# Attention units of 64 queries of two heads with 192 keys, in place of 128 queries of one head with 256

## The chip, the core and the metric

The kernel runs on one core of a Trainium2 chip. The core has five engines that run beside each other, each with its own queue: TensorE (PE, with its weight loads PEld), VectorE (DVE), ScalarE (ACT), GpSimd (POOL) and SyncE (SP), which issues the DMAs. The metric is the device time of one execution in microseconds (us); lower is better.

## The reference

A model of four layers over 1040 tokens (16 meta tokens and 1024 others) with 1024 features: sliding-window attention, mLSTM, HGRN2, and sliding-window attention again. Each layer adds its branch to the residual stream. The attention branch, which the change concerns, is, with 16 query heads, 4 key heads, head size 64, blocks of 128 queries and a window of 128 keys:

```python
s = jnp.einsum('bnqhgd,bnkhd->bnhgqk', qb, kk) * (A_HD ** -0.5)
dist = (jnp.arange(BLOCK)[:, None] + BLOCK) - jnp.arange(2 * BLOCK)[None, :]
band = (dist >= 0) & (dist < A_WIN)
s = jnp.where(mask[None, :, None, None], s, -jnp.inf)
m = jnp.maximum(s.max(axis=-1), sink)
e = jnp.exp(s - m[..., None])
p = e / (e.sum(axis=-1) + jnp.exp(sink - m))[..., None]
o = jnp.einsum('bnhgqk,bnkhd->bnqhgd', p, vv)
```

Here `kk` holds the 256 keys of a block and of the block ahead of it. Of these a query sees its own position and the 127 ahead of it; 64 neighbouring queries together see 191.

## The kernel before, in words

All layers hold the activations transposed: features on the partitions, tokens along the free dimension, in chunks of 400, 384 and 256 tokens (first chunk with the 16 meta tokens). Values are fp32; the large products are made of three `float32r` matmuls over a high and a low part (`split`, L193; `proj`, L211; `proj_out`, L293). Nine blocks cut the tokens: block 0 is the 16 meta tokens, blocks 1 to 8 have 128 tokens each.

*The order.* TensorE's order is written out by hand: every layer makes a list of steps (cost, function, early work), and `weave` (L56) lays two lists into each other by their costs, so that attention steps stand between projection matmuls. The costs are numbers in the code. The other engines' order is decided by a scheduler when the program is built; steps under `hi` (L286) have priority there.

*The attention layer* (`layer_a`, L416, for the first and the last layer). Queries of two heads come out of a projection in one tile t (64 features of each head on 128 partitions). `qk_proj` (L486) takes them through a scale, squares, a rotation by DMA and the rope; `stat_q` (L506) sums the squares of each query with one matmul per block (L516: 128 query columns as the stationary operand, 2 columns of ones moving), and ScalarE turns the sums into `rq` (L518, L519). `q_split` (L453) writes for each head a tile `qs` with the high part on one half of the partitions and the low part on the other (L463, L464).

`mixers` (L595) makes units out of (pair of tiles, block, head half hh). A unit holds two heads, u = 0 and 1, one from each tile of the pair, and has three steps, which run two units apart (`T_LAG`, `V_LAG`: T two and V four units behind S):

- `S_step` (L598): for each head two matmuls (keys' high and low part, L621 and L622) give scores of 128 queries by 256 keys, [128, 2, 256] in one PSUM bank. VectorE adds the mask, multiplies, and takes the minimum (L629), ScalarE takes the exponential and its sum (L632), VectorE the reciprocal (L634), GpSimd multiplies (L635). GpSimd also puts the sink into column 256 (L626).
- `T_step` (L638): four transposes (L647) turn the probabilities into a PSUM tile `pt` with the keys on the partitions; ScalarE copies the high part `Ph` (L649) and VectorE subtracts the low part `Pl` (L650).
- `V_step` (L652): four matmuls with the values (L666) add up in `po`; after two blocks ScalarE and VectorE put the two halves together (L674, L675).

*PSUM.* There are 8 banks of [128, 512] fp32. All PSUM tiles of all layers come out of `psum` (L145) with one tag and 8 buffers. Tiles named `pt` are those of T_step (L642), of the value tiles of the attention layers (L574), of `gate_turn` in the mLSTM layer, which turns the input and forget gates of a chunk one after the other (L785 to L794), of `s4` there, which turns back each block of a head with two transposes (L937) that VectorE copies out with two copies (L939), of a small turn at L829 and L830, and of the states of the HGRN2 layer (L1211).

Of the kernel before, what the change touches and what calls it, by code (L numbers as in the profile page):

```python
# [9 lines left out]
F32 = mybir.dt.float32  # L10
# [5 lines left out]
P = 128  # L16
# [95 lines left out]
def hybrid_kernel(ctx: ExitStack, tc: tile.TileContext, ins, out, layers=(0, 1, 2, 3)):  # L112
# [32 lines left out]
    def psum(tag, bufs):  # L145
        return ps.tile([P, 512], F32, tag="p", name=nm(tag), bufs=8)
# [269 lines left out]
    def layer_a(i, j, first, last, fin):  # L416
# [4 lines left out]
        def enter():  # L421
            R["mix"] = mix = new_mix()
            R["masks"] = masks = mix.tile([P, 384], F32, name=nm("masks"))
            sp.dma_start(masks, ins["a_masks"])
            R["cons"] = cons = mix.tile([P, 18], F32, name=nm("cons"))
            sp.dma_start(cons, ins["a_cols"][j])
            v.tensor_scalar(cons[:, 0:1], cons[:, 0:1], -0.125, None, op0=ALU.mult)
            v.tensor_scalar(cons[:, 2:18], cons[:, 2:18], -1.0, None, op0=ALU.mult)

        order = {}  # L430

# [21 lines left out]
        def q_split(t):  # L453


            def step(qf, n, c0, cn):
                def fn():
                    q = qf()
                    R["q", t, n] = []
                    for hh in range(2):  # L460
                        st = R["mix"].tile([P, CHUNKS[n][1]], F32R, tag=f"qs{n}", name=nm("qs"), bufs=4)
                        hs, os = slice(64 * hh, 64 * hh + 64), slice(64 - 64 * hh, 128 - 64 * hh)
                        s.copy(st[hs, :cn], q[hs])  # L463
                        v.tensor_tensor(st[os, :cn], q[hs], st[hs, :cn].bitcast(F32), op=ALU.subtract)  # L464
                        R["q", t, n].append(st)
# [20 lines left out]
        def qk_proj(src, gcol, work, fsplit, ch, t=None):  # L486
# [11 lines left out]
            def finish(n, c0, cn):  # L498
# [7 lines left out]
                def stat_q():  # L506

                    sq = late[n][1]
                    nb = len(CHUNK_BLOCKS[n])
                    R["rq", t, n] = rq = R["mix"].tile([P, 2 * nb], F32, tag=f"rq{n}", name=nm("rq"), bufs=4)  # L510
                    st = psa()
                    for k, b in enumerate(CHUNK_BLOCKS[n]):
                        if last and b == 0:
                            continue
                        q0 = blk(b)[0] - c0
                        pe.matmul(st[:, 2 * k : 2 * k + 2], sq[:, q0 : q0 + P], R["masks"][:, 0:P:64], start=True, stop=True)  # L516
                    z = slice(2 if last and n == 0 else 0, 2 * nb)
                    s.activation(rq[:, z], st[:, z], AF.Ln, bias=eps, scale=1.0 / 64)  # L518
                    s.activation(rq[:, z], rq[:, z], AF.Exp, scale=-0.5)  # L519
# [17 lines left out]
                if t is not None:  # L537
                    return [(D_Q[0], [0.0, factors, None]), (D_Q[1], [108 * len(CHUNK_BLOCKS[n]), stat_q, None]),
# [25 lines left out]
        def v_proj(src, jj):  # L564
# [7 lines left out]
            def finish(n, c0, cn):  # L572
                def fn():
                    pt = psum("pt", 1)  # L574
# [20 lines left out]
        def mixers():  # L595


            def S_step(w):  # L598
                mix, cons = R["mix"], R["cons"]
                b, hh, n = w["b"], w["hh"], w["n"]  # L600
                kh, kl = R["k", w["pair"] // 2][hh]
                q0, nq = blk(b)
                qb = slice(q0 - chunks[n][0], q0 - chunks[n][0] + nq)
                kq = CHUNK_BLOCKS[n].index(b)
                if b == 0:
                    k0, kbs = 0, ((0, 0, 16),)
                elif b == 1:
                    k0, kbs = 0, ((0, 0, 16), (1, 16, 128))
                else:
                    k0, kbs = q0 - P, ((b - 1, 0, 128), (b, 128, 128))  # L610
                w["kbs"] = kbs
                nk = sum(z[2] for z in kbs)
                kw, mo = (nk if b == 0 else 256), {0: 128, 1: 112}.get(b, 0)
                kb = slice(k0, k0 + kw)
                S = psum("pm", 2).rearrange("p (u k) -> p u k", u=2)
                w["Sm"] = Sm = mix.tile([P, 2, 257], F32, tag="Sm", name=nm("Sm"), bufs=2)
                st, den = small(2), small(2)
                sinks = []
                for u, t in enumerate(w["ts"]):
                    q = R["q", t, n][hh]  # L620
                    pe.matmul(S[:nq, u, :kw], q[:, qb], kh[:, kb], start=True, stop=False)  # L621
                    pe.matmul(S[:nq, u, :kw], q[:, qb], kl[:, kb], start=False, stop=True)  # L622
                    head = (2 * (t // 4) + hh) * 4 + t % 4
                    sinks.append(cons[:nq, 2 + head : 3 + head])
                    if u == 0:
                        g.tensor_copy(Sm[:nq, :, nk : nk + 1], cons[:nq, 2 + head : 4 + head].rearrange("p (u c) -> p u c", c=1))  # L626
                for u in range(2):
                    rq = R["rq", w["ts"][u], n][:nq, 2 * kq + hh : 2 * kq + hh + 1]
                    v.tensor_tensor_reduce(Sm[:nq, u, :nk], S[:nq, u, :nk], R["masks"][:nq, P + mo : P + mo + nk],  # L629
                                           rq, sinks[u], ALU.add, ALU.min, st[:nq, u : u + 1])  # L630
                for u in range(2):
                    s.activation(Sm[:nq, u, : nk + 1], Sm[:nq, u, : nk + 1], AF.Exp, scale=-1.0,  # L632
                                 bias=st[:nq, u : u + 1], accum_out=den[:nq, u : u + 1])
                v.reciprocal(den[:nq], den[:nq])  # L634
# [868 lines left out]
```

## Time and profile before

| | |
|---|---|
| Median of 3 runs | 2619.22 us (2617.09 to 2619.5) |
| The profiled execution | 2615.34 us, span of its instructions 2613.6 us |
| Granted TensorE clock, mean | 0.993 |
| Attention units, first layer and last layer | from 84 to 424 us and from 2213 to 2553 us |
| mLSTM layer alone on TensorE | from 523 to 1560 us |

The span goes from the first instruction's start to the last one's end. Rows of the groups read: line, engine, operation, tile written and tiles read, shapes, count, then busy time in us, mean ns of one, and the engine's idle time ahead of them with what ended it. A form as 128*128 128x256 on TensorE is the stationary operand (rows by columns) and the output. Rows of the timeline begin with the start in us and the duration in us. Rows of the waits read: who waited for whom, us in total, times, longest. A plain fp32 matmul (not `float32r`, not a transpose) leaves two records, an instruction of the others one. Matmuls are pipelined: the next one starts before the record of the one ahead ends, so that start to start is what one costs.

### The profile page before, as it was taken

The page shows a single profiled execution, that of the slowest core. Times are in us where ns is not written, and L with a number is a line of the kernel's source. Part 1 is how long each engine was busy: PE and PEld are TensorE (multiplying, and loading weights), DVE is VectorE, ACT ScalarE, POOL GpSimd, SP SyncE. Part 2 cuts the span into 40 slices and gives each one's busy share as a digit, 9 for nine tenths or more (in the row PEclk, how much of TensorE's full clock was granted, in tenths as well). Part 3 has the DMA queues.
Part 4 walks back from the last instruction along what each step waited for, and adds up shares of the span by engine and source line. Part 5 has one row for each costly group of instructions (what it writes and reads, how often), then busy time and mean ns, then how long its engine had stood idle before and what let it go on. Part 6 is the DMA issues. An engine that isn't in the chain of part 4 may idle for free.

```text
span 2613.6 us, 54261 instructions
## 1 busy us (share of the span) xinstructions
PE 2565.6 (98%) x20422; PEld 2485.5 (95%) x20422; DVE 1952.1 (75%) x5248; ACT 1689.4 (65%) x4422; POOL 249.1 (10%) x502
## 2 busy tenths in 40 slices
PE   7999999999999999999999999999999999999999
PEld 6999999999999999999999999999999999999999
DVE  6797798785647474646465688988888978887996
ACT  6776767576555555554555757878675857767772
POOL 2221221000000000000000000101000000321330
PEclk8999999999999999999999999999999999999999
DMA  4212111021111111111111111111111113112112
GB/s 130 68 51 85 54 44 48 22 66 58 41 58 41 58 41 51 44 53 41 57 41 50 57 32 37 34 34 34 38 38 31 37 51 92 56 47 84 56 40 79
DMA packets 82582, 135.92 MB, mean 52 GB/s; under 512 B 12032, under 2 KB 35712, under 8 KB 82320
## 3 DMA queue, kind: packets, MB, share of 16 engines
q1 hardware_dynamic: 82320, 132.45, 16.3%
q8 instruction: 161, 2.64, 0.4%
q14 instruction: 101, 0.83, 0.1%
HBM read 117.56 MB, written 4.26 MB: 47 GB/s over the span
## 4 chain that ended last, share of the span: by engine, by line
PE 80%; DVE 9%; ACT 6%; DMA 2%; issue 2%; SPq 1%; POOL 0%; DVEq 0%; ACTq 0%; POOLq 0%
PE pj L228 39%; PE pj L322 16%; PE pj L277 10%; PE po L666 2%; PE pt L647 2%; PE po L909 1%; PE pa L923 1%; PE po L911 1%; PE pm L621 1%; ACT Sm L632 1%; PE pm L622 1%; DVE Sm L629 1%; PE pj L273 1%; PE pm L1161 1%; DMA cs<-in_rope 1%
## 5 line engine op out<-in xcount | busy, mean ns | idle before, releaser
L228 PE MATMUL pj<-uh,wh 128*128 128x256 f32 (+2 forms) x2688 | 915.2, 340 | 9.3 <-ACT uh L194 9.2
L228 PE MATMUL pj<-ul,wh 128*128 128x256 f32 (+2 forms) x2688 | 867.7, 323 | 2.1 <-DVE ul L195 1.9
L228 PE MATMUL pj<-uh,wl 128*128 128x256 f32 (+2 forms) x2688 | 864.6, 322 | 0.0
L228 PEld LDWEIGHTS pj<-uh,wh 128*128 128x128 f32 x2688 | 510.0, 190 | 26.0 <-ACT uh L194 12.5
L228 PEld LDWEIGHTS pj<-ul,wh 128*128 128x128 f32 x2688 | 510.1, 190 | 10.5 <-DVE ul L195 5.4
L228 PEld LDWEIGHTS pj<-uh,wl 128*128 128x128 f32 x2688 | 509.7, 190 | 0.0
L195 DVE TENSOR_TENSOR wl<-wr,wh 128x512 fp32r<-128x512 f32 (+1 forms) x338 | 233.6, 701 | 50.1 <-ACT wh L194 47.1
L194 ACT CAST wh<-wr 128x512 fp32r<-128x512 f32 (+1 forms) x338 | 202.9, 613 | 102.1 <-PE pj L322 32.7
L322 PE MATMUL pj<-yh,wh 128*128 128x384 f32 (+2 forms) x768 | 253.2, 330 | 8.2 <-DVE x L325 6.2
L325 DVE TENSOR_TENSOR x<-x,pj 128x384 f32<-128x384 f32 (+2 forms) x480 | 234.6, 507 | 35.0 <-PE pj L322 33.7
L322 PE MATMUL pj<-yh,wl 128*128 128x384 f32 (+2 forms) x768 | 245.5, 320 | 0.0
L322 PE MATMUL pj<-yl,wh 128*128 128x384 f32 (+2 forms) x768 | 245.5, 320 | 0.0
L277 PE MATMUL pj<-wh,uh 128*128 128x256 f32 (+1 forms) x768 | 232.2, 302 | 0.0
L277 PE MATMUL pj<-wl,uh 128*128 128x256 f32 (+1 forms) x768 | 216.5, 282 | 0.0
L277 PE MATMUL pj<-wh,ul 128*128 128x256 f32 (+1 forms) x768 | 216.2, 282 | 0.0
L635 POOL TENSOR_TENSOR Sm<-Sm,s 128x512 f32<-128x512 f32 (+2 forms) x136 | 142.2, 1046 | 450.6 <-DVE s L634 435.8
L632 ACT ACTIVATE Sm<-Sm,s 128x257 f32<-128x257 f32 (+2 forms) x272 | 130.8, 482 | 78.9 <-DVE s L629 74.7
L404 ACT ACTIVATE t<-t 128x384 f32<-128x384 f32 (+2 forms) x240 | 117.9, 491 | 82.9 <-DVE t L403 80.8
L403 DVE SCALAR_TENSOR_TENSOR t<-pj,t 128x384 f32<-128x384 f32 (+2 forms) x192 | 98.7, 514 | 80.1 <-ACT t L402 78.4
L322 PEld LDWEIGHTS pj<-yh,wh 128*128 128x128 f32 x768 | 144.5, 188 | 11.9 <-DVE x L325 7.3
L194 ACT CAST yh<-r 128x384 fp32r<-128x384 f32 (+2 forms) x120 | 57.1, 478 | 152.0 <-PE pj L322 139.9
L277 PEld LDWEIGHTS pj<-wh,uh 128*128 128x128 f32 x768 | 144.6, 188 | 2.2
(255 smaller groups left out, 5434.0 us busy)
## 6 DMA issues: line engine op xcount, KB each, us to landing
wr<-in_b_win SPq DMA_DIRECT2D x124, 256.0 KB, 2.9
wr<-in_a_win SPq DMA_DIRECT2D x80, 256.0 KB, 2.9
wr<-in_c_win SPq DMA_DIRECT2D x64, 256.0 KB, 2.7
wr<-in_a_wout SPq DMA_DIRECT2D x32, 256.0 KB, 2.8
wr<-in_b_wout SPq DMA_DIRECT2D x32, 256.0 KB, 2.8
t<-t SPq DMA_DIRECT2D x104, 48.0 KB, 1.9
cs<-in_rope SPq DMA_DIRECT2D x11, 400.0 KB, 3.4
cs<-in_rope SPq DMA_DIRECT2D x11, 384.0 KB, 3.4
```

Source lines behind the costliest of these rows:

```text
L194: s.copy(h, src)
L195: v.tensor_tensor(l, src, h.bitcast(F32), op=ALU.subtract)
L228: pe.matmul(acc[:, :cn], a[:, k, :], b[:, k, c0 : c0 + cn], start=(k == 0 and i == 0), stop=(k == KT - 1 and i == 2))
L277: pe.matmul(acc[:cn, :nc], a[:, k, c0 : c0 + cn], m[:, kk, :], start=(k == 0 and j == 0), stop=(k == KT - 1 and j == 2))
L322: pe.matmul(acc[:, :cn], a[:, k, mc], b, start=(k == 0 and i == 0), stop=(k == 1 and i == 2))
L325: v.tensor_tensor(x[:, m, c0 : c0 + cn], x[:, m, c0 : c0 + cn], acc[:, :cn], op=ALU.add)
L403: v.scalar_tensor_tensor(a[:, :cn], z, 0.0, a[:, :cn], op0=ALU.min, op1=ALU.subtract)
L404: s.activation(a[:, :cn], a[:, :cn], AF.Exp)
L632: s.activation(Sm[:nq, u, : nk + 1], Sm[:nq, u, : nk + 1], AF.Exp, scale=-1.0, bias=st[:nq, u : u + 1], accum_out=den[:nq, u : u + 1])
L635: g.tensor_tensor(Sm[:nq, :, :nk], Sm[:nq, :, :nk], den[:nq].rearrange("p (u c) -> p u c", c=1).to_broadcast([nq, 2, nk]), op=ALU.mult)
L647: pe.transpose(pt[:kn, ki, u, :nq], Sm[:nq, u, ko : ko + kn], ident[:nq, :nq])
L666: pe.matmul(po[:, :, q0 - g0 : q0 - g0 + nq], V[pair // 2, kb][:kn, P * hh : P * hh + P], w[part][:kn, ki, :, :nq], start=(ki == 0 and par ...
```

## The change

A unit still has two heads, but its rows are now 64 queries of both heads, and its two halves are a = 0 and 1, the first and the last 64 queries of the block. Half a keeps the 192 keys from 128 ahead of its first query on. `q_split` interleaves the two heads by 64 queries in one tile per pair, `stat_q` works by half blocks (64 stationary columns) and writes to partitions 0 to 63 or 64 to 127 by the parity of t, and the sinks and masks are laid out for it. The score matmuls take 256 keys where they exist; the columns that are not used are overwritten or not read. The transposes put the keys of both halves on the partitions of the blocks b - 1 and b; rows that no half sees are zero, from a clearing of `pt` and of two fixed `Sm` tiles at the layer's start. So `pt` in the attention layers is one fixed tile, and `psum` gives the tag `pt` a bank of its own and all others 7. The value tiles' turn uses `psa` instead.

```diff
     def psum(tag, bufs):
-        return ps.tile([P, 512], F32, tag="p", name=nm(tag), bufs=8)
+        if tag == "pt":
+            return ps.tile([P, 512], F32, tag="pt", name=nm(tag), bufs=1)
+        return ps.tile([P, 512], F32, tag="p", name=nm(tag), bufs=7)
...
+            R["pt"] = psum("pt", 1)
+            v.memset(R["pt"], 0.0)
+            R["Sm"] = [mix.tile([P, 2, 257], F32, name=nm("Sm")) for _ in range(2)]
+            for z in R["Sm"]:
+                g.memset(z, 0.0)
...
+                        parts = [(st[:, :ce].rearrange("p (h u q) -> p h u q", u=2, q=64)[:, :, u],
+                                  q[:, meta:].rearrange("p (h q) -> p h q", q=64))]
+                        if meta:
+                            parts.append((st[:, ce + 64 * u : ce + 64 * u + meta], q[:, :meta]))
+                        for z, src in parts:
+                            s.copy(z[hs], src[hs])
+                            v.tensor_tensor(z[os], src[hs], z[hs].bitcast(F32), op=ALU.subtract)
...
-                        pe.matmul(st[:, 2 * k : 2 * k + 2], sq[:, q0 : q0 + P], R["masks"][:, 0:P:64], start=True, stop=True)
...
+                    for k, q0 in enumerate(hv):
+                        pe.matmul(st[us, 2 * k : 2 * k + 2], sq[:, q0 - c0 : q0 - c0 + 64], R["masks"][:, 0:P:64], start=True, stop=True)
...
-                    return [(D_Q[0], [0.0, factors, None]), (D_Q[1], [108 * len(CHUNK_BLOCKS[n]), stat_q, None]),
+                    return [(D_Q[0], [0.0, factors, None]), (D_Q[1], [108 * len(halves(n)), stat_q, None]),
...
-                    pt = psum("pt", 1)
+                    pt = psa()
...
+                for a in range(na):
+                    qa = 2 * (q0 + 64 * a - blk(CHUNK_BLOCKS[n][1 if n == 0 else 0])[0]) if b else 768
+                    qb = slice(qa, qa + nr)
+                    k0, at, kw = q0 + 64 * a - 192, 256 * a, 256
+                    if b < 2:
+                        k0, at, kw = 0, 256 * a + lo[a], 256 - lo[a]
+                    elif k0 < 0:
+                        k0, at = k0 + 64, at + 64
+                    pe.matmul(S[:nr, at : at + kw], q[:, qb], kh[:, k0 : k0 + kw], start=True, stop=False)
+                    pe.matmul(S[:nr, at : at + kw], q[:, qb], kl[:, k0 : k0 + kw], start=False, stop=True)
+                for a in range(na):
+                    c = 2 * hv.index(q0 + 64 * a) + hh
+                    m0 = P + (P if b == 0 else lo[a] - 64)
+                    v.tensor_tensor_reduce(Sm[:nr, a, lo[a] : 256], S[:nr, 256 * a + lo[a] : 256 * a + 256],
+                                           R["masks"][:nr, m0 : m0 + 256 - lo[a]], rq[:nr, c : c + 1],
+                                           sink[:nr], ALU.add, ALU.min, st[:nr, a : a + 1])
...
+                pt = R["pt"].rearrange("p (k a q) -> p k a q", k=2, a=2)
...
+                    parts = [(0, 0, 64, 128), (0, 1, 0, 128)]
+                if b:
+                    parts += [(1, 0, 192, 64), (1, 1, 128, 128)]
+                for ki, a, z, m in parts:
+                    nr = P if b else 64 + NMETA
+                    pe.transpose(pt[:m, ki, a, :nr], Sm[:nr, a, z : z + m], ident[:nr, :nr])
...
+                            pe.matmul(po[:, z0 : z0 + 256], V[pair // 2, kb][:, P * hh : P * hh + P],
+                                      w[part][:, ki], start=(ki == 0 and part == "Ph"), stop=(ki == 1 and part == "Pl"))
```

For blocks 2 to 8 `lo` is (64, 64), so 192 columns of each half are reduced, exponentiated and multiplied; for block 1 it is (176, 112).

More of the change, by code (lines that the diff above doesn't have):

```diff
@@ L611, in S_step @@
[L611 to L616, printed above, removed]
-                st, den = small(2), small(2)
[L618 to L633, printed above, removed]
```

127 lines of the change are left out of this document (70 added, 57 removed).

## The prediction

> **What bounds the kernel now.** I read the page first, then the busy time by stage, then the list of groups with shapes kept apart, then who waited for whom, then the timeline at the places that the diff touches.
>
> ```profile
> span 2613.6 us, 54261 instructions
> ...
> PE 2565.6 (98%) x20422; PEld 2485.5 (95%) x20422; DVE 1952.1 (75%) x5248; ACT 1689.4 (65%) x4422; POOL 249.1 (10%) x502
> ...
> PE 80%; DVE 9%; ACT 6%; DMA 2%; issue 2%; SPq 1%; POOL 0%; DVEq 0%; ACTq 0%; POOLq 0%
> ```
>
> TensorE is busy for 98% and holds 80% of the chain that ended last. So work that is taken from VectorE, ScalarE or GpSimd is worth only what TensorE waits for them, and every wait that TensorE newly gets is paid in full, where it had none. Which of the two holds is read stage by stage (stretch, its length, then PE, PEld, DVE, ACT, POOL busy):
>
> ```profile
> 84.00:490.00 406.00, 399.44 (x2754) 388.21 (x2753) 347.72 (x917) 286.16 (x812) 93.31 (x155) 1.00 0.18 54
> 523.00:1560.00 1037.00, 1036.92 (x6836) 1011.29 (x6835) 644.07 (x1617) 582.98 (x1375) 7.54 (x67) 1.00 0.15 49
> 2213.00:2560.00 347.00, 336.56 (x2343) 330.43 (x2342) 291.25 (x753) 249.07 (x697) 87.26 (x127) 0.99 0.20 60
> ```
>
> The first and the third stretch hold the attention units of the two attention layers: there TensorE idles 6.6 and 10.4 us, 17.0 together, beside a VectorE that is 86% and 84% busy. That is all the room that faster softmax steps have. The middle stretch is the mLSTM layer: TensorE idles 0.08 us in 1037. The diff seems not to touch that layer, but it changes the pool of PSUM banks that it draws from.
>
> **What the change takes away.** A score tile goes from 2x256 to 2x192 keys for VectorE's masked reduction (L629), ScalarE's exponential (L632) and GpSimd's product (L635).
>
> ```profile
> L629 DVE CUSTOM_DVE_ANT_0 Sm<-pm,masks,cons 128x256 f32<-128x256 f32 x224 | 113.7, 539 | 5.0 <-PE pm L622 4.2
> ...
> L629 DVE CUSTOM_DVE_ANT_0 Sm<-pm,masks,cons 128x144 f32<-128x144 f32 x32 | 12.3, 420 | 2.9 <-PE pm L622 2.9
> ```
>
> (mean 539 and 420 ns), and on GpSimd:
>
> ```profile
> L635 POOL TENSOR_TENSOR Sm<-Sm,s 128x512 f32<-128x512 f32 x112 | 126.1, 1126 | 273.7 <-DVE s L634 265.8 <-PE pt L647 5.4 <-PE pm L622 2.2
> ```
>
> 112 columns cost VectorE 539 - 420 = 119 ns, so 64 fewer save 68 ns, times 224 instructions 15 us; ScalarE's exponential loses the same 64 columns; GpSimd's 1126 ns falls by a quarter at most, some 30 us over 112. All three are off the path. Per unit the chain from scores to transposes gets 2x68 + 280 = 0.4 us shorter and a little on ScalarE, against waits of this size:
>
> ```profile
> PE pt L647 <- POOL Sm L635: 2.5, 4, 1.2
> ```
>
> ```profile
> PE po L666 <- DVE v L587: 4.3, 2, 3.6
> ```
>
> The first row (first attention stretch) is the wait that the shorter chain ends; the second (last layer's start) hangs on the value tiles, which no softmax step makes. Bounds: nothing to all 17.0 us. I take 5 us off, because 15 us less in 639 us of VectorE work shortens a queue by 2%, and only the waits on L635 hang on the chain itself.
>
> TensorE itself gets nothing from the 192 keys: the score matmuls are still 4 a unit with 256 keys swept (`kw` is 256), the transposes are still 4, and the product with the values is still 4 times 256 columns. The few matmuls of the meta block and of block 1 differ by under 0.5 us.
>
> **What it adds on TensorE: the query statistic** (`stat_q`, L516). Before, one matmul per block with 128 stationary columns, 136 in all; after, one per half block with 64 columns, 8x17 + 8x16 = 264. An fp32 matmul leaves two records, so 272 records become 528.
>
> ```profile
> L516 PE MATMUL pa<-masks,t 128*128 128x2 f32 x272 | 34.5, 242 | 0.1
> ```
>
> ```profile
> 111.81 0.95 PE L516 MATMUL pa<-masks,t 128*128 128x2 f32 x8
> ```
>
> ```profile
> 84.66 0.17 PE L621 MATMUL pm<-r,qs 128*16 128x16 f32 x1
> ...
> 84.69 0.17 PE L622 MATMUL pm<-r,qs 128*16 128x16 f32 x1
> ```
>
> Eight records with 128 columns take 0.95 us from the first start to the last end, and a short matmul lasts 0.17 (the two rows above): (0.95 - 0.17) / 7 = 112 ns from start to start. With 16 columns it is 84.69 - 84.66 = 30 ns. On the line between them, 64 columns come to 30 + 48/112 x 82 = 65 ns: 528 x 65 = 34.3 us against 272 x 112 = 30.5, so 3.8 us more. Bounds: 528 x 30 = 15.8 (14.7 less) and 528 x 112 = 59.1 (28.6 more). I take the line, because what sets the pitch of so short a matmul is the load of its stationary columns, and that goes from 93 to 198 ns over the same columns, not in one step:
>
> ```profile
> L516 PEld LDWEIGHTS pa<-masks,t 128*128 128x128 f32 x272 | 36.8, 198 | 0.4 <-ACT t L493 0.4
> ...
> L621 PEld LDWEIGHTS pm<-r,qs 128*16 128x16 f32 x16 | 1.4, 93 | 2.3 <-DVE Pl L650 2.0 <-DVE x L325 0.3
> ```
>
> The Trainium skill (TensorE: Matmul & The Clock Gate, LDWEIGHTS) gives a load as its columns over 1.2 GHz, an estimate of 53 ns for 64; by it the sum would be 528 x 53 = 28 us, 2.5 us less instead of 3.8 more. The 112 ns row agrees with its 107 for 128 columns; no row here has 64.
>
> Entering a narrow fp32 matmul costs something of its own. Between two L228 matmuls lie 0.12 us here, ahead of the 16-column L888 0.21, so 0.09 more; ahead of the 8-column transposes of L793 there is the usual 0.18:
>
> ```profile
> 553.33 0.28 PE L228 MATMUL pj<-ul,wh 128*128 128x256 f32 x1
> 553.45 0.28 PE L228 MATMUL pj<-uh,wl 128*128 128x256 f32 x1
> 553.66 0.21 PE L888 MATMUL pm<-q,r 128*16 128x16 f32 x2
> ```
>
> ```profile
> 519.43 0.35 PE L228 MATMUL pj<-ul,wh 128*128 128x400 f32 x1
> 519.61 0.34 PE L228 MATMUL pj<-uh,wl 128*128 128x400 f32 x1
> 519.79 0.27 PE L793 MATMUL pt<-ident,G 128*8 128x128 f32 x1
> ```
>
> `stat_q` runs 48 times (8 tiles, 3 chunks, 2 layers): 48 x 0.09 = 4.3 us, bounds 0 and twice that, if leaving costs as much. I take 4.3. The 64-column transposes of T_step (one in four, 128 units) I cost at nothing, by the L793 row; their upper bound is the first rival below.
>
> **What it adds in waits: one bank for all transposes.** Before, a `pt` took any of 8 banks. Now every `pt` of the kernel, in the mLSTM and HGRN2 layers too, shares one bank, and each fill must wait for the last reader of the one ahead. The wait sits in TensorE's own queue, so all matmuls stand behind it. The trace of before shows how early each fill came.
>
> In the mLSTM layer, `gate_turn` (L793) fills two in a row, three times. The second fill starts at 520.01 while ScalarE still reads the first until 520.73 + 0.46 = 521.19, and at 503.71 against 503.83 + 0.58 = 504.41:
>
> ```profile
> 520.01 0.09 PEld L793 LDWEIGHTS pt<-ident,G 128*8 128x8 f32 x1
> ...
> 520.73 0.46 ACT L794 ACTIVATE r<-pt,bbias 8x256 f32<-8x256 f32 x1
> ```
>
> ```profile
> 503.71 0.31 PEld L793 LDWEIGHTS pt<-ident,G 16*8 16x8 f32 x4 [0.22 <-issue]
> ...
> 503.83 0.58 ACT L794 ACTIVATE r<-pt,bbias 8x400 f32<-8x400 f32 x1
> ```
>
> These are 1.18 and 0.70 us; three at their mean are 2.8. At the end of each head, block 7 and block 8 are turned back (L937) with one step between them. At 744.94 the second starts, and VectorE copies out the first until 745.30 + 0.88/2 = 745.74:
>
> ```profile
> 744.94 0.38 PE L937 MATMUL pt<-ident,hn 128*128 128x128 f32 x2
> ...
> 745.30 0.88 DVE L939 COPY r<-pt 128x128 f32<-128x128 f32 x4
> ```
>
> That is 0.80 us, and the pattern comes once per head: 8 x 0.80 = 6.4 us. Since the middle stretch has no idle time, nothing absorbs these 9.2 us. Bounds: 6 (half of the heads free) and 15 (1.5 us a head).
>
> In the attention layers T_step waits for VectorE's subtraction (L650) of the unit before. Mostly it ends in time; where VectorE is behind, it does not:
>
> ```profile
> 2254.78 0.63 PE L647 MATMUL pt<-ident,Sm 128*128 128x128 f32 x4
> ...
> 2255.03 0.68 DVE L650 TENSOR_TENSOR Pl<-pt,Ph 128x512 fp32r<-128x512 f32 x1
> ```
>
> This unit starts 2255.03 + 0.68 - 2254.78 = 0.93 us before the subtraction of the unit ahead of it ends. Of the 134 neighbouring pairs in the timeline 8 are late, two more by as much and the rest by under 0.3, 3.8 us together; with VectorE a little faster I take 3, bounds 0 and 10.
>
> Last, all other tiles share 7 banks in place of 8. TensorE already ran into the limit where VectorE adds the outputs late:
>
> ```profile
> 1560.84 0.28 PE L322 MATMUL pj<-yh,wh 128*128 128x256 f32 x1
> ...
> 1562.20 0.55 DVE L325 TENSOR_TENSOR x<-x,pj 128x384 f32<-128x384 f32 x1
> ...
> 1562.80 0.39 PE L322 MATMUL pj<-yh,wh 128*128 128x256 f32 x1 [1.45 <-DVE x L325]
> ```
>
> With one bank fewer the matmuls at 1560.84 wait as well, and TensorE comes out one tile later, up to 0.75 us. Some four such places: 3 us, bounds 0 and 10.
>
> **What it moves.** Query copies go into one interleaved tile per pair, as many elements as before, with 32 small extra copies on ScalarE and VectorE in the first layer; both are hidden behind TensorE. The sink's copy on GpSimd waits for the exponential two units back, which ends before the transposes it waited for. The DMA queues issue the same transfers. `stat_q` has twice its cost in the weave of steps, which shifts attention steps by a few projection matmuls; I cost that at 0, give or take 4 us.
>
> **The sum.** The profiled execution took 2615.3 us (span 2613.6): + 3.8 + 4.3 + 2.8 + 6.4 + 3 + 3 - 5 = + 18.3, 2633.6 us. It lies 3.9 below the median of the runs, 2619.2; on that scale the forecast is 2637.5, and I say 2637.
>
> **The rivals**, on the same scale.
>
> *The mode switch drains.* If each 64-column transpose pays on entering and on leaving what L888 pays, 128 x 2 x 0.09 = 23 us come on top: 2660. For it: L888. Against it: L793 is a transpose and enters free. The Trainium skill (TensorEngine Tiling, Key Properties) says that changing the tiling mode drains the engine, and lists column tiling as disabling the fp32 transpose mode; that speaks against this change, and the L793 row disagrees with it. Chance 0.12.
>
> *The attention stages lose their waits: faster.* If what holds TensorE there is the softmax chain and VectorE's backlog, and a few per cent less work lets both catch up, the 17.0 us of idle time go and the new T_step wait and the bank shortage with them, with the statistic at equal cost: + 9.2 - 17.0 = - 7.8, 2611. It decides once T_step's inputs are ready ahead of TensorE in every unit. Against it: the larger wait row belongs to the value tiles. Chance 0.13.
>
> *Nothing to measure.* The built order places the readers so that the one bank is free in time, and the statistic is paid by its narrower loads: 2615 to 2624. Against it: the built program of the changed kernel has a wait for VectorE and ScalarE on the second turning of each head, with 6 matmuls between the two. Chance 0.13.
>
> *The forecast*, one bank and more statistic matmuls on a full TensorE: 0.62.
>
> **How the numbers follow.** Range: the likeliest case goes from 2622 to 2655 with its bounds (not all at one end at once); taking in the drain's price to 2660 and part of the faster cases, 2612 to 2660 leaves out some 0.2. A measurement of this kernel can tell 0.2%, 5 us, from no change. Faster by that: 0.13; within: 0.14 (the third rival and a small part of the forecast); slower: 0.73.
>
> **What would show it.** In the mLSTM stretch TensorE's idle time rises from 0.08 to some 9 us, with waits of the `hn` transposes for VectorE (7 or 8 times 0.8) and of the `G` transposes for ScalarE (3 times 0.9). The statistic shows 528 records about 65 ns apart and 0.21 us ahead of the first. In the attention stretches the `pt` transposes wait for `Pl`, and idle time is near 17 us still. Reductions over 192 columns take some 470 ns. The prediction is wrong if the mLSTM stretch stays without idle time, if groups of four transposes last longer than 0.60 us, or if the attention stretches lose most of their idle time.

## The result, and the profile after

| | before | after |
|---|---|---|
| Median, us | 2618.52 (4 runs, 2617.09 to 2619.50) | 2631.93 (4 runs, 2631.24 to 2633.61) |
| Ratio | | 1.0053, 95% interval 1.0035 to 1.0070 |
| Profiled execution, span, us | 2613.6 | 2629.8 |

The change costs 13.4 us by the medians and 16.2 by the spans of the two profiled executions. It is slower, by more than the 0.2% that a measurement can tell; 2637 was forecast, with a range of 2612 to 2660.

The page of the changed kernel, the lines that answer to those shown of before:

```profile
span 2629.8 us, 54928 instructions
...
PE 2575.5 (98%) x20654; PEld 2487.5 (95%) x20654; DVE 1937.3 (74%) x5250; ACT 1687.4 (64%) x4422; POOL 220.6 (8%) x514
...
PE 80%; DVE 10%; ACT 5%; DMA 3%; issue 2%; POOL 0%; SPq 0%; DVEq 0%; POOLq 0%; ACTq 0%
```

VectorE, ScalarE and GpSimd together are 45 us less busy (14.8, 2.0 and 28.5), and the execution is longer: their work was not the bound. TensorE is 10 us busier, and 6 us of new idle time make up the rest. The busy time by stage tells where the idle time is (stretch, its length, then PE, PEld, DVE, ACT, POOL busy):

```profile
84.00:490.00 406.00, 399.70 (x2808) 388.81 (x2808) 335.65 (x907) 281.92 (x803) 78.14 (x161) 1.00 0.18 54
523.00:1560.00 1037.00, 1029.29 (x6778) 1002.58 (x6777) 633.30 (x1591) 580.06 (x1365) 6.95 (x65) 1.00 0.16 49
1585.00:2120.00 535.00, 529.08 (x6916) 506.74 (x6915) 458.56 (x1509) 406.21 (x1161) 45.55 (x124) 1.00 0.12 36
2213.00:2560.00 347.00, 340.57 (x2459) 330.17 (x2458) 285.23 (x760) 250.26 (x706) 70.21 (x127) 1.00 0.21 63
```

The mLSTM stretch, which no edited step touches, now has 1037.00 - 1029.29 = 7.7 us without TensorE work, where it had 0.08. The two attention stretches have 6.3 and 6.4, 12.7 together, where they had 17.0. The waits of TensorE in the mLSTM stretch, all of them (who waited for whom, us in total, times, longest; before, this list was empty):

```profile
PE pt L966 <- DVE r L968: 5.9, 5, 1.5
PE pt L822 <- ACT r L823: 0.9, 1, 0.9
PE pm L917 <- DVE r L890: 0.9, 1, 0.9
```

L966 is the `hn` turn at a head's end (L937 before), L822 the `G` turn of `gate_turn` (L793 before). The timeline at the first `hn` wait shows what is waited for:

```profile
754.04 0.48 DVE L968 COPY r<-pt 128x128 f32<-128x128 f32 x2
754.64 0.20 PEld L966 LDWEIGHTS pt<-ident,hn 128*128 128x128 f32 x2 [1.84 <-ACT t L403]
754.67 0.41 PE L966 MATMUL pt<-ident,hn 128*128 128x128 f32 x2 [1.54 <-DVE r L968]
```

VectorE's two copies out of the bank end at 754.52, and only then do the next two transposes get into it. Nothing of the model's arithmetic asks for this order: the two turns belong to different blocks and only share a bank.

Following the same instructions through both traces (the `G` turn, the add of the mLSTM output, the `kT` product of the HGRN2 layer; their rows before are 503.71 and 1562.80 in the prediction and the first here, the others are those of after) gives the account by layer:

```profile
2109.09 0.49 PE L1221 MATMUL pa<-v,kT 128*128 128x128 f32 x2 [1.16 <-ACT kT L1213]
```

```profile
507.49 0.31 PEld L822 LDWEIGHTS pt<-ident,G 16*8 16x8 f32 x4 [0.97 <-ACT r L823]
...
1575.64 0.39 PE L324 MATMUL pj<-yh,wh 128*128 128x256 f32 x1 [1.80 <-DVE x L327]
...
2124.38 0.49 PE L1250 MATMUL pa<-v,kT 128*128 128x128 f32 x2 [1.41 <-ACT kT L1242]
```

Later by 3.8, 12.8, 15.3 and, at the end, 16.2 us: 3.8 came with the first attention layer and the first gate turn, 9.1 with the rest of the mLSTM layer, 2.5 with HGRN2, 0.9 with the last attention layer. Most of the loss lies in layers whose code is the same.

### The profile page after: what moved, and what is told of

It reads as the page before. It is cut to its first block, busy times and chain, and to the rows that moved or that the text cites. A ratio compares the mean times of both kernels' runs of the same rounds, so it can differ in the third digit from the quotient of the medians.

```text
span 2629.8 us, 54928 instructions
## 1 busy us (share of the span) xinstructions
PE 2575.5 (98%) x20654; PEld 2487.5 (95%) x20654; DVE 1937.3 (74%) x5250; ACT 1687.4 (64%) x4422; POOL 220.6 (8%) x514
## 3 DMA queue, kind: packets, MB, share of 16 engines
q1 hardware_dynamic: 82320, 132.38, 16.2%
## 4 chain that ended last, share of the span: by engine, by line
PE 80%; DVE 10%; ACT 5%; DMA 3%; issue 2%; POOL 0%; SPq 0%; DVEq 0%; POOLq 0%; ACTq 0%
PE pj L230 39%; PE pj L324 15%; PE pj L279 10%; PE po L694 2%; PE pt L668 2%; DVE wl L197 1%; PE po L938 1%; DMA wr<-in_b_win 1%; PE pa L952 1%; PE pa L537 1%; PE po L940 1%; PE pm L640 1%; PE pm L639 1%; PE pj L275 1%; PE pm L1190 1%
## 5 line engine op out<-in xcount | busy, mean ns | idle before, releaser
L648 ACT ACTIVATE Sm<-Sm,s 128x193 f32<-128x193 f32 (+3 forms) x264 | 115.5, 439 | 78.3 <-DVE s L644 77.0
L279 PEld LDWEIGHTS pj<-wl,uh 128*128 128x128 f32 x768 | 144.7, 188 | 1.9
```

Of the source, the lines that this page charges most:

```text
L279: pe.matmul(acc[:cn, :nc], a[:, k, c0 : c0 + cn], m[:, kk, :], start=(k == 0 and j == 0), stop=(k == KT - 1 and j == 2))
L648: s.activation(Sm[:nr, a, lo[a] : 257], Sm[:nr, a, lo[a] : 257], AF.Exp, scale=-1.0, bias=st[:nr, a : a + 1], accum_out=den[:nr, a : a + 1])
```

## The experiments

The theory was that of the forecast, the bank and the statistic on a TensorE that is full. The main rivals were that only one of the two counts, and that the units themselves (a shorter softmax, one held `pt` tile) gain or lose. All ratios are to the kernel before, run on the same chip in five rounds each; its medians there were 2617.0 to 2617.8 us. Differences between two edited kernels are differences of their medians.

| kernel | median, us | ratio, 95% interval |
|---|---|---|
| b_bank: before, banks split 1 + 7 | 2632.74 | 1.0057 (1.0044 to 1.0069) |
| b_pt2: before, banks split 2 + 6 | 2631.71 | 1.0050 (1.0037 to 1.0063) |
| b_seven: before, 7 shared banks | 2623.50 | 1.0023 (1.0013 to 1.0033) |
| b_half: before, half-block statistic, halves alternate | 2615.85 | 0.9991 (0.9982 to 1.0000) |
| b_rows: the same, halves one after the other | 2619.49 | 1.0009 (1.0000 to 1.0018) |
| b_soft: before, 192 of 256 columns in the softmax | 2614.77 | 0.9992 (0.9983 to 1.0001) |
| a_mend: after, 8 shared banks | 2620.04 | 1.0007 (0.9998 to 1.0015) |
| a_stat: after, whole-block statistic | 2630.35 | 1.0045 (1.0032 to 1.0059) |
| a_mend_stat: after, both | 2617.59 | 0.9996 (0.9987 to 1.0005) |
| a_mend_alt: a_mend, alternating half statistic | 2617.53 | 1.0000 (0.9991 to 1.0009) |
| a_free: a_mend_alt, no held `pt` | 2613.09 | 0.9984 (0.9975 to 0.9993) |
| a_sweep: after, scores over 192 keys | 2653.96 | 1.0135 (1.0119 to 1.0150) |

Two cautions for all of them. The build orders VectorE and ScalarE anew for every kernel. TensorE's order of steps stays (a few HGRN2 records that change places aside), but when VectorE's sequences of two traces are aligned by operation and tile, some 55 to 160 of 5248 instructions stand elsewhere in most of these kernels, some 150 in b_soft, and 300 in a_sweep. And the granted clock ahead of the first attention unit is not the same in every trace: from 20 to 40 and from 40 to 60 us it was 0.98 and 0.83 in that of before, 0.83 and 0.74 in b_seven's, 0.91 and 0.74 in b_soft's, and these two are 4.1 and 4.0 us late at 84 us already. Differences of 1 or 2 us are not to be read as the edit's own.

**b_bank, the bank alone.** The value tiles' turn also uses `psa`, as in the change.

```diff
-        return ps.tile([P, 512], F32, tag="p", name=nm(tag), bufs=8)
+        if tag == "pt":
+            return ps.tile([P, 512], F32, tag="pt", name=nm(tag), bufs=1)
+        return ps.tile([P, 512], F32, tag="p", name=nm(tag), bufs=7)
```

> The kernel before, with only the banks as the change has them: the tag pt has one bank of its own, all else seven. Theory (the bank is the larger part of the loss): the mLSTM stretch gets the 7 to 8 us of idle time that the changed kernel shows there (waits of the hn and G transposes), the attention layers 2 to 5 more for transposes that wait for the reader before: 2628 to 2634, +10 to +15. Rival (the statistic is what costs, the waits at the bank are taken back by later waits that shrink): 2617 to 2621, and TensorE's idle time in the mLSTM stretch stays under 2 us.

2632.74: 15.0 over before, as much as the whole change. TensorE's busy time in the mLSTM stretch, and its waits there:

```profile
523.00:1560.00 1037.00, 1028.95 (x6770) 1001.92 (x6769) 632.09 (x1588) 581.02 (x1367) 6.95 (x65) 1.00 0.15 49
```

```profile
PE pt L939 <- DVE r L941: 6.2, 6, 1.6
PE pt L795 <- ACT r L796: 0.9, 1, 0.9
PE pm L890 <- DVE r L863: 0.9, 1, 0.9
```

8.0 us without work, and the same three waits as in the changed kernel. The bank by itself makes the loss of the layers between. The rival falls.

**a_mend, the change without its bank.** One tag, eight buffers; the attention layers still hold their `pt` tile from entering to the end, and give it back then.

```diff
-        if tag == "pt":
-            return ps.tile([P, 512], F32, tag="pt", name=nm(tag), bufs=1)
-        return ps.tile([P, 512], F32, tag="p", name=nm(tag), bufs=7)
+        return ps.tile([P, 512], F32, tag="p", name=nm(tag), bufs=8)
```

> The changed kernel with one tag and eight banks for all; the attention's pt tile is held from entering an attention layer to its end and returned then, so that the mLSTM and HGRN2 layers have their eight banks again. Theory: idle time of the mLSTM stretch back to about 0.1 us, 2619 to 2624, 8 to 13 under the changed kernel. Rival (the statistic alone costs the 13): 2630 to 2634.

2620.04, 11.9 under the changed kernel and hardly over before. The mLSTM stretch is full again:

```profile
523.00:1560.00 1037.00, 1037.00 (x6835) 1012.05 (x6834) 644.04 (x1615) 584.82 (x1377) 7.07 (x66) 1.00 0.15 49
```

**a_stat and a_mend_stat, the statistic.** One matmul with 128 columns for a block, as before; ScalarE's Ln, in two instructions for one, puts the halves of the result where the units want them. a_mend_stat has both mendings.

```diff
-                    for k, q0 in enumerate(hv):
-                        pe.matmul(st[us, 2 * k : 2 * k + 2], sq[:, q0 - c0 : q0 - c0 + 64], R["masks"][:, 0:P:64], start=True, stop=True)
-                    s.activation(rq, st[us, : 2 * len(hv)], AF.Ln, bias=eps[us], scale=1.0 / 64)
+                    for k, b in enumerate(bs):
+                        q0 = blk(b)[0]
+                        pe.matmul(st[:, 2 * k : 2 * k + 2], sq[:, q0 - c0 : q0 - c0 + P], R["masks"][:, 0:P:64], start=True, stop=True)
+                    for a in range(2):
+                        ha = slice(64 * a, 64 * a + 64)
+                        dst = rq[:, 2 * m :].rearrange("p (k a h) -> p k a h", a=2, h=2)[:, :, a]
+                        s.activation(dst, st[ha, 2 * m : 2 * m + w].rearrange("p (k h) -> p k h", h=2), AF.Ln, bias=eps[ha], scale=1.0 / 64)
```

> The changed kernel with the statistic of the queries by whole blocks again: one matmul with 128 columns of sq for a block, and the two heads' halves put where the units want them by the Ln activations (two for one). Theory (528 loads 58 ns apart against 272 of 103, and entries of 0.09 more): 5 to 8 under the changed kernel, 2624 to 2627. Rival (the bank is all of it): 2630 to 2633.

> Both mendings in one: eight banks for the layers between, and the statistic by whole blocks. Theory: what is left of the change is the units themselves; if the two costs are independent and explain the loss, 2612 to 2618, 14 to 20 under the changed kernel, level with the kernel before or up to 5 under it. Rival (the units themselves cost: single pt tile, more transposes in series, 192-key tails): 2621 to 2628.

a_stat comes to 2630.35, 1.6 under the changed kernel, a_mend_stat to 2617.59, 2.5 under a_mend; in neither pair do the intervals part. The theory of 5 to 8 us falls for a_stat. Yet TensorE did get the time back. Summed from each record's start to the next one's, the statistic takes 27.2 us in a_stat and 36.4 in the changed kernel; the steps ahead of its 48 groups, each from the start of the matmul ahead of the group to the group's first start, take another 7.8 and 11.6. That is 35.0 against 48.0, and by the two pages TensorE is 11.6 us less busy. Where it went is in the attention stretches of a_stat:

```profile
84.00:490.00 406.00, 396.56 (x2721) 387.71 (x2720) 338.02 (x912) 289.41 (x830) 77.68 (x161) 1.00 0.18 54
...
2213.00:2560.00 347.00, 336.64 (x2346) 329.78 (x2345) 287.78 (x761) 257.48 (x729) 70.43 (x127) 0.99 0.21 63
```

They idle 9.4 + 10.4 = 19.8 us, against 12.7 in the changed kernel: some 7 of the 11.6 us turn into waiting there, some 3 in other places, and 1.7 reach the span. The statistic's matmuls fill idle time that the attention stretches have anyway. With both mendings the time is level with before: the units by themselves neither gain nor lose (the statistic's doubled cost in the weave is still in this kernel, so its shift of the steps is part of that zero), and bank and statistic, 11.9 + 2.5 = 14.4, account for the 13.4.

**b_half and b_rows, what a half-block load costs.** b_half is the kernel before with 64-column matmuls, the halves of a block one after the other; b_rows has the same matmuls, all first halves of a group ahead of all second halves (the two loops exchanged).

```diff
-                        pe.matmul(st[:, 2 * k : 2 * k + 2], sq[:, q0 : q0 + P], R["masks"][:, 0:P:64], start=True, stop=True)
+                        for a in range(2):
+                            us = slice(64 * a, 64 * a + 64)
+                            pe.matmul(st[us, 2 * k : 2 * k + 2], sq[:, q0 + 64 * a : q0 + 64 * a + 64], R["masks"][:, 0:P:64], start=True, stop=True)
```

> The kernel before with only the statistic as the change has it, 64 columns of sq for a load and the results on the two halves of the partitions (544 matmuls for 272). Theory: 544 times 58 to 65 ns against 272 times 103 to 112, with entries of 0.09 more for 48 groups: +6 to +9, 2624 to 2628. Rival (loads hide beside other matmuls): within 2 of the kernel before.

> The kernel before with the half-block statistic, the same 544 matmuls as in b_half, but all of a group's first halves ahead of all its second halves. In b_half, where the halves alternate, the second of a pair starts 5 ns after the first in 270 of the pairs and the statistic lasts 21.6 us in sum, start to next start (27.8 before, 36.4 in the changed kernel). Theory (two loads run beside each other when they go to different halves of the array's columns, and not on the same half): starts 58 to 60 ns apart again, 33 to 37 us in sum, as in the changed kernel; of the 12 to 15 us more on TensorE some 2 to 5 show in the time: 2617 to 2622. Rival (what made b_half fast is its place beside other matmuls): 22 us in sum, and the time of b_half.

b_half is not slower but, if anything, faster, by 1.9 us at the edge of its interval. The theory of 6 to 9 more falls; the rival's number (within 2) holds, but not its reason, since the statistic's records take less time on TensorE, 21.6 us for 27.8. The steps ahead of its groups take back most of that, 12.2 us for 7.0, so that 33.7 stand against 34.9 in all. The 1.9 us need not be the statistic's: the mean granted clock was 0.9936 over the runs of b_half and 0.9924 over those of before beside them, and among the latter 0.001 more clock goes with some 1.7 us less. Here is one group in the timeline of before, of the changed kernel, of b_half and of b_rows (start, duration), for before and b_half with the matmul ahead of it:

```profile
111.69 0.28 PE L622 MATMUL pm<-r,qs 128*128 128x256 f32 x1
111.81 0.95 PE L516 MATMUL pa<-masks,t 128*128 128x2 f32 x8
```

```profile
113.80 0.98 PE L537 MATMUL pa<-masks,t 128*64 128x2 f32 x14
```

```profile
112.27 0.28 PE L624 MATMUL pm<-r,qs 128*128 128x256 f32 x1
112.47 0.63 PE L518 MATMUL pa<-masks,t 128*64 128x2 f32 x16
```

```profile
115.08 0.89 PE L518 MATMUL pa<-masks,t 128*64 128x2 f32 x16
```

Ahead of a group of 64-column matmuls the step is 0.21 us (the median of 48, in all three kernels), ahead of the 128-column ones of before 0.12. In the changed kernel a group writes one half of the partitions (the parity of t decides which), and 14 records start 58 ns apart after a first step of 79: 0.079 + 12 x 0.058 + 0.198 = 0.97. In b_half neighbours write different halves, which is not what the change does: the starts come in pairs 5 to 7 ns apart, and 16 records take the time of 8. In b_rows, within this group of 16 the first four and the last four start singly and the eight between them in interleaved pairs, twelve steps for 16: 0.89. So 64-column matmuls that write different halves of the partitions run beside each other, on the same half they don't, and, as the starts read, TensorE begins on the second half while three records of the first are still to start. In sum the statistic's records take 27.5 us in b_rows, where 33 to 37 were expected, and 22 by the rival: the reach ahead puts it between. With the steps ahead of its groups it takes 39.2, 4.3 more than before, and the time, 2619.49, is 2.3 more and in the theory's range. The Trainium skill (TensorE: Matmul & The Clock Gate, Part 3: Packing small matmuls) says that small matmuls run at once when each puts its output on partitions of its own, about 4 ns from start to start; the 5 to 7 ns here are near that. The same section says that matmuls start strictly in order, which the pairs in the middle of b_rows' groups don't fit, if they are what their starts suggest.

**b_seven and b_pt2, which property of the bank costs.** Seven buffers for all under one tag; and two banks for `pt`, six for the rest (as b_bank with `bufs=2` and `bufs=6`).

```diff
-        return ps.tile([P, 512], F32, tag="p", name=nm(tag), bufs=8)
+        return ps.tile([P, 512], F32, tag="p", name=nm(tag), bufs=7)
```

> The kernel before with seven banks in place of eight, shared by all as before. Tells the loss of a bank from the tag of one bank. Theory (what costs is that two pt tiles in a row want the same bank): +1 to +4, 2619 to 2623, with little idle time in the mLSTM stretch. Rival (seven are too few, however they are shared): as much as the bank of its own, +9 to +15.

> The kernel before with the banks parted six and two: the tag pt has two of its own. Theory (what costs in the mLSTM and HGRN2 layers is that a pt tile waits for the reader of the one just before): with two banks TensorE's idle time in the mLSTM stretch falls under 2 us, and the loss is about that of seven shared banks: 2620 to 2626. Rival (any fixed split of the banks costs alike): 2629 to 2634, with idle time of 5 or more there.

The mLSTM stretch, first of b_seven, then of b_pt2:

```profile
523.00:1560.00 1037.00, 1036.95 (x6834) 1011.48 (x6833) 640.86 (x1608) 583.71 (x1375) 6.96 (x65) 1.00 0.16 49
```

```profile
523.00:1560.00 1037.00, 1035.98 (x6827) 1011.11 (x6827) 641.71 (x1610) 584.62 (x1375) 7.02 (x65) 1.00 0.16 49
```

Both are full there: the idle time of this layer needs a tag with a single bank. But the total tells more. Seven shared banks cost 5.7 us, somewhat over what the theory gave. Not all of it need be the bank's: of the 8.5 us that its trace is late, 4.1 stand at 84 us already, at the lower clock named above. 2.3 come at the end of the first attention layer and 0.8 where the mLSTM output is added, both beside waits for VectorE's adds, the place that the prediction named. Two and six cost 14.5, as the rival had it, though not where it had it: the loss moves. Against before, the same instructions come 4.2 us late at the end of the mLSTM layer, 13.7 at the end of HGRN2 and 16.7 at the end of the program. New waits stand in HGRN2, of which before has none:

```profile
PE pa L1260 <- DVE t L413: 1.6, 1, 1.6
...
PE pj L230 <- ACT v L245: 1.0, 1, 1.0
PE pj L230 <- DVE S L1230: 0.8, 1, 0.8
```

There, it seems, the six banks for all other tiles run short; the wait names a reader, not the bank. Whichever way the eight are split, some layer needs the one that the other tag has.

**b_soft, the shorter softmax alone.** Reduction, exponential and product go over the last 192 of 256 columns from block 2 on; the first 64 columns are left out of the softmax and hold zeros, so the kernel computes something else there. TensorE's work is as before.

```diff
-                    v.tensor_tensor_reduce(Sm[:nq, u, :nk], S[:nq, u, :nk], R["masks"][:nq, P + mo : P + mo + nk],
+                    v.tensor_tensor_reduce(Sm[:nq, u, z0:nk], S[:nq, u, z0:nk], R["masks"][:nq, P + mo + z0 : P + mo + nk],
```

> The kernel before with the masked reduction, the exponential and the product on the last 192 of the 256 columns alone (blocks from the third on; the first 64 columns are left out of the softmax and hold zeros, TensorE's work is as before). Measures what the shorter softmax alone is worth. Theory of the forecast (-5: the attention stretches keep most of their 17 us of idle time, which later steps end): 2612 to 2616. The rival that the attention stretches lose their waits: 2601 to 2606.

2614.77, about 3 under before, with an interval that just reaches no change. The attention stretches idle 5.2 + 7.9 = 13.0 us, 4 less than before:

```profile
84.00:490.00 406.00, 400.84 (x2760) 391.09 (x2758) 336.87 (x914) 283.72 (x816) 78.60 (x151) 1.00 0.19 55
...
2213.00:2560.00 347.00, 339.12 (x2367) 334.12 (x2367) 286.88 (x762) 247.85 (x705) 71.94 (x125) 0.99 0.21 61
```

That is near the forecast's 5, and not the rival's 17; its trace, 4.0 us late at 84 us, gains 4.9 from there to the end. VectorE was reordered too (some 150 instructions), so that the gain may be the order's as well; this stays open.

**a_sweep, scores over 192 keys.** The change still sweeps 256 keys on TensorE; this sweeps only those that a half sees.

```diff
-                    k0, at, kw = q0 + 64 * a - 192, 256 * a, 256
+                    k0, at, kw = q0 + 64 * a - 128, 256 * a + 64, 192
```

> The changed kernel with the score matmuls sweeping only the 192 keys that a half of a block sees, in place of 256. Theory of the forecast (under 256 columns a float32r matmul takes about two cycles a column, as the rows of 144 and 80 columns show, 333 and 215 ns): 896 matmuls at 320 to 440 ns against about 220: far slower in the attention stretches, +20 and more above the changed kernel. Rival (it goes by columns at one cycle, and is bound by the weight load): 2628 to 2632, level or some us faster.

2653.96, 22.0 over the changed kernel: the size of the theory, but not its reason. The mean of a 192-column matmul falls (first the changed kernel, then a_sweep), and the starts are 110 to 112 ns apart instead of 118:

```profile
L639 PE MATMUL pm<-r,qs 128*128 128x256 f32 x224 | 59.2, 287 | 0.0
L640 PE MATMUL pm<-r,qs 128*128 128x256 f32 x224 | 57.8, 280 | 0.0
```

```profile
L638 PE MATMUL pm<-r,qs 128*128 128x192 f32 x224 | 56.4, 277 | 0.0
L637 PE MATMUL pm<-r,qs 128*128 128x192 f32 x224 | 55.2, 272 | 0.0
```

So 192 columns cost no more than 256; that theory falls. It had read a rate out of the mean durations of the first matmul of a pair in block 1 (333 and 215 ns for 144 and 80 columns); the second ones, of the same widths, last 288 and 292 in the same trace. What is new is idle time in the attention stretches, 29.0 us for 12.7, and one wait:

```profile
PE pt L666 <- DVE Pl L671: 22.1, 29, 2.0
```

T_step waits for the subtraction of the unit ahead, 29 times, where the changed kernel does it twice for 1.3 us. TensorE's order is the same, the sums on VectorE are no larger, but VectorE's order in the attention layers is another. That the order is the cause is argued from this, not shown.

**a_mend_alt and a_free, toward a better version.** a_mend_alt takes b_half's alternating matmuls into a_mend_stat. a_free also drops the held `pt`: every unit takes one of the eight shared banks. For that all of the tile must be written, so the second row of keys is turned from 128 columns that run on over zeros in `Sm`, and the first half's sink column stands ahead of its window. (A first form of it, a_best, with rows of 320 columns in `Sm`, has no time: its tiles take 34.4 kb per partition, and 33.5 were left.)

```diff
-                pt = R["pt"].rearrange("p (k a q) -> p k a q", k=2, a=2)
+                pt = psum("pt", 1).rearrange("p (k a q) -> p k a q", k=2, a=2)
...
-                    parts += [(1, 0, 192, 64), (1, 1, 128, 128)]
+                    parts += [(1, 0, 192, 128), (1, 1, 128, 128)]
```

> The changed kernel with eight shared banks outside the attention layers (as in a_mend) and the statistic of both halves of a block by alternating 64-column matmuls (as in b_half), the two heads put in their places by the Ln activations (as in a_mend_stat). Theory (the statistic takes 6 us less of TensorE than by whole blocks, of which the attention layers pass on a third): 2614 to 2617, under a_mend_stat by 1 to 3. Rival (the waits there take it up): 2617 to 2619, as a_mend_stat.

> As a_mend_alt, and no held pt tile: each unit takes a bank of the shared eight. The tile needs no zeros of its own, since the second row of keys is turned from 128 columns that run on into columns of Sm which hold zeros, and the sink column of the first half stands ahead of its window instead of behind it. Theory (the held bank, seven for the rest and the waits for Pl are what the units lose in the attention layers, so that the shorter softmax can show): 2610 to 2615, under the kernel before by 3 to 7. Rival (the attention layers are bound elsewhere, the waits only change their names): 2615 to 2619, no difference from a_mend_alt.

a_mend_alt, 2617.53, is a_mend_stat again, as its rival had it. The 6 us that its theory counted on are not there: the records take 6.4 less than in a_mend_stat, but with the steps ahead of the groups the statistic takes 33.5 us for 35.3. a_free comes to 2613.09: 4.4 under a_mend_alt, which ran on another chip, though the two intervals still touch, and 4 under before with an interval (0.9975 to 0.9993) that leaves no change out. A part of the 4 may be the clock's: its mean over the runs was 0.9933, and 0.9923 over those of before beside them. The transposes' waits, a_mend_alt and then a_free (which has no such wait for `Pl` at all):

```profile
PE pt L677 <- DVE Pl L682: 3.4, 7, 1.2
PE pt L677 <- POOL Sm L661: 3.4, 4, 1.9
```

```profile
PE pt L681 <- POOL Sm L663: 4.9, 6, 1.9
```

So the units of 64 queries by 192 keys seem to be worth a little, 0.16%, once no bank is kept from the others.

## Why the prediction was right, and where not

Direction, place and range were right: the loss is that of the bank, in the mLSTM layer above all. The terms:

- *The `hn` turns, 6.4.* Right in place and in sum. 5.9 us in 5 waits, 1.2 each, where 8 of 0.80 were worked out: three heads show no wait, the others wait longer. That the two make up for each other is luck. b_bank has 6.2 without any other edit.
- *The gate turns, 2.8.* Right in size. Over the whole trace the changed kernel has 2.3 us in 3 such waits (b_bank the same), the last of them in the mLSTM stretch.
- *T_step's waits, 3.* Too much: 1.3 in 2 waits (list over the whole trace, below). But the held tile may cost in other ways: without it a_free is 4.4 lower.

```profile
PE pt L668 <- POOL Sm L652: 2.7, 3, 2.0
PE pt L822 <- ACT r L823: 2.3, 3, 0.9
...
PE pt L668 <- DVE Pl L673: 1.3, 2, 1.1
```

- *Seven banks, 3.* Right in place, its size is not settled: b_seven costs 5.7, and its trace shows 3.1 at two such places. At the one named, the adding of the mLSTM output at 1562.80, TensorE waits for 1.80 instead of 1.45, in b_seven and in the changed kernel.
- *The bank together* was 15.2; it measures 15.0 alone (b_bank) and 11.9 inside the change (a_mend).
- *The statistic, 3.8 + 4.3.* This is the term that failed. The step that failed is to add it in full as work on a full TensorE. Its groups lie in and ahead of the attention stretches, where 17.0 us of idle time stood by the prediction's own table, and they filled that: 1.6 to 2.5 us reached the end. Its TensorE time was mis-sized as well, and too low: the records rose from 27.8 to 36.4 us, 8.6 for the 3.8, and the steps ahead of the groups from 7.0 to 11.6, 4.6 for the 4.3, 13 in all for 8.1. For before, 30.5 was worked out and 27.8 measured: in most groups the first step is some 30 ns and only the others 112, and the last record lasts 0.25 us, not the 0.17 that was taken, so that 112 came out by two slips that cancel. For after, 34.3 was worked out: most steps are 58 ns and not 65, but the first of a group is 80, some within it are 110, and the one that leaves it is 128. By the Trainium skill's estimate of 53 ns for a 64-column load (TensorE: Matmul & The Clock Gate, LDWEIGHTS) the matmuls would have cost 28 us; the 58 ns are nearer to it than to 65, the 36.4 are not.
- *The shorter softmax, -5.* About right in size, if at all: b_soft has -3, reaching 0. The attention stretches' idle time fell from 17.0 to 12.7, where "near 17 still" was written; it was the statistic that filled it (19.8 in a_stat), not the softmax that ended it.

The sum, 18.3, is 5 more than the 13.4 measured, mostly the statistic's 6; what the other terms miss about cancels.

The rivals: *the mode switch* is out for the transposes. The 64-column ones last as long as the others in the changed kernel, the starts in a group are 109 ns apart in the median, and the 128 groups of four take 0.60 us in the median and 0.61 in the mean, in before as after. (The prediction's sign, longer than 0.60, was too tight: its own row of before has 0.63.)

```profile
L668 PE MATMUL pt<-ident,Sm 128*128 128x128 f32 x352 | 72.6, 275 | 1.7 <-DVE Pl L673 1.3 <-POOL Sm L652 0.3
...
L668 PE MATMUL pt<-ident,Sm 128*64 128x128 f32 x128 | 35.0, 274 | 0.0
```

```profile
199.72 0.60 PE L668 MATMUL pt<-ident,Sm 128*128 128x128 f32 x4
```

*The attention stages lose their waits* is out by b_soft and a_mend_stat: a quarter of the idle time at most. *Nothing to measure* was half right: the statistic is nearly free, though by idle time and not by narrower loads, and the single bank is not.

VectorE's reductions came as worked out (539 - 68 = 471):

```profile
L644 DVE CUSTOM_DVE_ANT_0 Sm<-pm,masks,cons 128x192 f32<-128x192 f32 x224 | 99.0, 473 | 4.8 <-PE pm L640 3.6
```

## What to carry to other kernels

Before giving a tile a bank of its own, look at every other place that takes its tag: a pool that all layers share charges the price where TensorE has no idle time, not where the edit is. Extra work on the bounding engine is to be charged stage by stage as well: beside existing idle time 13 us of it cost some 2 here. If a matmul must be cut into narrow ones, let neighbours write different partitions, so that they run side by side, and count the step ahead of each group too: in groups of 8 to 16 records it took back most of the gain.

## What the runs showed of the hardware

- 64-column fp32 matmuls that alternate between output partitions 0 to 63 and 64 to 127 start in pairs 5 to 7 ns apart: 16 records in 0.63 us, against 0.98 for 14 that all write the same half.
- Ahead of a group of 64-column fp32 matmuls the step from the last other matmul is 0.21 us, ahead of 128-column ones 0.12 (medians of 48 groups, changed kernel and before).
- As the starts read, TensorE begins on the other half while three of eight records on this one are still to start (b_rows, 16 records in 0.89 us).
- 192 moving columns of `float32r` start 110 to 112 ns apart, 256 columns 118: nearly the same, and no slower.
- A 128-row transpose with 64 stationary columns costs the same as one with 128 (274 and 275 ns, starts 109 ns apart in the median), with no gap on entering or leaving.
